# A sparse 3x3 convolution: the fifth image pair's load in two parts, later half loads moved by one or two blocks

## Chip, cores and metric

The kernel runs on one core of one Trainium2 chip. The metric is device time in microseconds (us) of the whole kernel, median over the runs.

## The reference

A 3x3 convolution with padding 1 over 16 images of 64 channels and 64 x 64 pixels, to 128 output channels. The weights are 90% zeros, but the kernel treats them as dense; what is computed is

```python
x_pad = np.pad(x, ((0, 0), (0, 0), (1, 1), (1, 1)))
for b, co, ci, kh, kw:   # x (16, 64, 64, 64) float32, weight (128, 64, 3, 3)
    output[b, co] += weight[co, ci, kh, kw] * x_pad[b, ci, kh:kh+64, kw:kw+64]
```

## The kernel before

**Pairs and blocks.** Images go in pairs: the 64 channels of two images fill 128 partitions, so there are NP = 8 pairs. A pair's 64 output rows are cut into BLOCKS = 4 blocks of ROWS = 16, which makes N = 32 blocks, counted k = 0 to 31; pair p is blocks 4p to 4p + 3. For each block three small bf16 tiles are made from the input rows: `odd` (the nine odd rows around the block, copied by ScalarE, ACT), `even` (nine even rows, by GpSimd, POOL) and `sums` (eight sums of an even and the next odd row, POOL). With weight combinations prepared at the start, TensorE makes three products of them per block: `ps[0]` from `sums` (6 matmuls), `ps[1]` from `odd` (12) and `ps[2]` or `ps[3]` from `even` (12). ACT copies `ps[0]` to `pc`; VectorE (DVE) adds `pc` to the other two and writes even and odd output rows in float32 (L288, L292).

**Loads.** Apart from the first 32 rows of pair 0, which SyncE (SP) loads in float32 at the start (L97), all input is loaded by POOL (L102), cast from float32 to bf16 on the way. `PIECES[p]` says in which row ranges a pair is loaded, each with its own semaphore `s_x[p][i]`; a fill waits for the semaphores of the rows that it reads (L118 to L153). Pair 0's rest and pairs 1 to 3 are loaded at the start. `WHEN` (L43) maps a block number k to a piece: POOL's program is one list, and behind `sums` and `even` of block k it issues that piece (L268). Pairs 3 to 7 have an input buffer of their own, so that no load waits for a buffer. From block 2 on POOL works up to two blocks ahead of TensorE: before it fills the tiles of block k it waits until TensorE is done with those of block k - 2 (L266).

**Stores.** SP stores a pair's float32 output (4 MB) when DVE is done with the pair's four blocks, pairs 6 and 7 (`HALVED`) in halves of 2 MB (L298 to L308); the very last half is issued behind the main section (L353). There are four output buffers, so DVE waits for the store of pair p - 4 before it writes pair p (L285). At the end SP waits for the semaphores of the last stores (L355).

**Order.** TensorE runs blocks in order (a loop over 16 turns of two blocks, L338 to L348); all other engines have their orders written out. A few lines carry what the change touches:

```python
    PIECES = {p: [(0, H)] for p in range(NP)}
    PIECES[0] = [(HEAD, H)]
    for p in (5, 6, 7):
        PIECES[p] = [(0, HALF * 4), (HALF * 4, H)]
    WHEN = {4: (4, 0), 7: (5, 0), 10: (5, 1), 13: (6, 0), 16: (6, 1), 20: (7, 0), 24: (7, 1)}
```

Of the kernel before, what the change touches and what calls it, by code (L numbers as in the profile page):

```python
# [16 lines left out]
HALF = 8  # L17
# [5 lines left out]
def kernel(  # L23
# [7 lines left out]
    B, C_IN, H, W = x.shape  # L31
    C_OUT, _, KH, KW = weight.shape
    assert (B, C_IN, H, W) == (16, 64, 64, 64) and (C_OUT, KH, KW) == (128, 3, 3)
    NP = B // 2
    HEAD = 32
    N = NP * BLOCKS
    HALVED = (6, 7)

    PIECES = {p: [(0, H)] for p in range(NP)}
    PIECES[0] = [(HEAD, H)]  # L40
    for p in (5, 6, 7):
        PIECES[p] = [(0, HALF * 4), (HALF * 4, H)]
    WHEN = {4: (4, 0), 7: (5, 0), 10: (5, 1), 13: (6, 0), 16: (6, 1), 20: (7, 0), 24: (7, 1)}  # L43

    def sbuf(name, shape, dtype):
        return nc.alloc_sbuf_tensor(name, shape, dtype).ap()
# [1 line left out]
    def sem(name):  # L48
        return nc.alloc_semaphore(name)
# [31 lines left out]
    s_st = [sem(f"s_st{p}") for p in range(NP)]  # L81
# [18 lines left out]
    def load(p, i=0):  # L100
        a, b = PIECES[p][i]
        nc.gpsimd.dma_start(out=xs[p][:, a:b, :], in_=pair(p)[:, a:b, :]).then_inc(s_x[p][i], 16)  # L102
# [160 lines left out]
    for k in range(1, N):  # L263
        for fill_in, product in ((fill_sums, 2), (fill_even, 6)):
            if k >= UNROLL:
                wait(g, s_pe, 6 * (k - UNROLL) + product)  # L266
            fill_in(k)
        if k in WHEN:  # L268
            load(*WHEN[k])

# [9 lines left out]
    for k in range(N):  # L280
        p, b = divmod(k, BLOCKS)
# [15 lines left out]
    s = nc.sync  # L297
# [55 lines left out]
    nc.sync.dma_start(out=into(NP - 1, H // 2, H), in_=outs[(NP - 1) % 4][:, :, H // 2 : H, :])  # L353
    with tc.tile_critical(no_gpsimd_drain=True):
        for p in range(4, NP):  # L355
            s.wait_ge(s_st[p], 16)


# [28 lines left out]
```

## Time and profile before

| | |
|---|---|
| median of 3 runs | 126.75 us (126.66 to 131.19) |
| the profiled execution | 127.12 us, of which the span from first to last instruction is 125.3 us |
| TensorE matmul busy | 110.2 us (88%), granted clock 0.962 of full speed on average |
| VectorE, POOL, ACT busy | 82.6, 63.8, 54.6 us |
| the eleven loads by POOL | 0.5 to 0.7 us of POOL each to issue; 7.8 to 19.7 us from issue to landing, the six half loads of pairs 5 to 7 12.2 us in the median |
| the stores by SP | issued at 23.1, 36.1, 49.0, 62.0, 74.9, 87.9, 94.4, 100.9, 107.4 and 114.1 us; 4 MB ones 19.2 us to landing in the median |

How to read it: busy times are those of one profiled execution, in us; the span's slices are forty equal stretches of 3.1 us, a digit is the busy share in tenths. DMA is the mean busy share of the core's 16 DMA engines, and GB/s counts the bytes that they wrote: a load that casts float32 to bf16 counts half of what it reads. "SPq" is a DMA issue in SP's queue.

### The profile page before, as it was taken

The page shows a single profiled execution, that of the slowest core. Times are in us where ns is not written, and L with a number is a line of the kernel's source. Part 1 is how long each engine was busy: PE and PEld are TensorE (multiplying, and loading weights), DVE is VectorE, ACT ScalarE, POOL GpSimd, SP SyncE. Part 2 cuts the span into 40 slices and gives each one's busy share as a digit, 9 for nine tenths or more (in the row PEclk, how much of TensorE's full clock was granted, in tenths as well). Part 3 has the DMA queues.
Part 4 walks back from the last instruction along what each step waited for, and adds up shares of the span by engine and source line. Part 5 has one row for each costly group of instructions (what it writes and reads, how often), then busy time and mean ns, then how long its engine had stood idle before and what let it go on. Part 6 is the DMA issues. An engine that isn't in the chain of part 4 may idle for free.

```text
span 125.3 us, 2489 instructions
## 1 busy us (share of the span) xinstructions
PE 110.2 (88%) x983; PEld 57.3 (46%) x983; DVE 82.6 (66%) x74; ACT 54.6 (44%) x78; POOL 63.8 (51%) x88
## 2 busy tenths in 40 slices
PE   5969999999999999999999999999999999990000
PEld 2425555555555555555555555555555555540000
DVE  0575777777777777777777777777777777773000
ACT  4525555555555555544444444444444555530000
POOL 4457557557557557556755575557555555100000
PEclk9999999999999999999999999999999999999555
DMA  3999999999999999999999999999999999999990
GB/s 110 354 221 225 215 217 212 209 165 364 379 373 362 408 331 381 392 356 364 394 371 332 430 426 345 341 436 434 362 339 413 424 408 429 429 429 421 432 408 21
DMA packets 4595, 42.79 MB, mean 342 GB/s; under 512 B 368, under 2 KB 368, under 8 KB 1392
## 3 DMA queue, kind: packets, MB, share of 16 engines
q1 hardware_dynamic: 3008, 34.90, 66.2%
q0 software_dynamic: 1584, 7.87, 31.5%
q14 instruction: 3, 0.02, 0.0%
HBM read 17.07 MB, written 33.55 MB: 404 GB/s over the span
## 4 chain that ended last, share of the span: by engine, by line
PE 82%; DVE 2%; issue 0%; DVEq 0%
PE ps L320 82%; DVE home L288 1%; DVE home L292 1%; DVEq L143 0%
## 5 line engine op out<-in xcount | busy, mean ns | idle before, releaser
L275 ACT COPY pc<-ps 128x1024 f32<-128x1024 f32 x32 | 32.4, 1012 | 51.9 <-PE ps L320 51.9
L320 PE MATMUL ps<-odd,wT 64*128 64x504 bf16 (+1 forms) x384 | 47.3, 377 | 0.0
L320 PE MATMUL ps<-even,wT 64*128 64x504 bf16 (+1 forms) x384 | 47.3, 377 | 0.0
L288 DVE TENSOR_TENSOR o<-ps,pc 128x1024 f32<-128x1024 f32 x24 | 29.4, 1225 | 19.6 <-PE ps L320 19.6
L320 PEld LDWEIGHTS ps<-even,wT 64*128 64x128 bf16 x384 | 22.0, 94 | 19.5
L320 PEld LDWEIGHTS ps<-odd,wT 64*128 64x128 bf16 x384 | 21.9, 94 | 19.5
L292 DVE TENSOR_TENSOR o<-ps,pc 128x1024 f32<-128x1024 f32 x24 | 29.4, 1224 | 0.0
L320 PE MATMUL ps<-sums,wT 64*128 64x504 bf16 (+1 forms) x192 | 26.5, 377 | 0.9 <-PEq L331 0.9
L180 POOL TENSOR_TENSOR sums<-x 128x512 bf16<-128x512 bf16 x20 | 23.1, 1157 | 0.1
L169 POOL COPY even<-x 128x576 bf16<-128x576 bf16 (+1 forms) x20 | 13.0, 649 | 19.2 <-PE ps L320 19.2
L320 PEld LDWEIGHTS ps<-sums,wT 64*128 64x128 bf16 x192 | 10.9, 94 | 11.0 <-issue 1.4
L180 POOL TENSOR_TENSOR sums<-home 128x512 bf16<-128x512 bf16 (+1 forms) x11 | 13.3, 1213 | 3.2 <-DMA home<-in_x_dram 3.1
L288 DVE TENSOR_TENSOR home<-ps,pc 128x1024 f32<-128x1024 f32 x8 | 9.8, 1225 | 6.4 <-PE ps L320 6.4
L160 ACT COPY odd<-x 128x576 bf16<-128x576 bf16 (+1 forms) x20 | 13.2, 661 | 0.0
L169 POOL COPY even<-home 128x576 bf16<-128x576 bf16 (+2 forms) x11 | 6.7, 609 | 8.2 <-PE ps L320 8.2
L292 DVE TENSOR_TENSOR home<-ps,pc 128x1024 f32<-128x1024 f32 x8 | 9.8, 1224 | 0.0
L170 POOL MEMSET even<- 128x64 bf16 x8 | 1.2, 151 | 10.8 <-PE ps L320 10.8
L236 PE MATMUL ps<-idle_rhs 128*128 128x512 bf16 x14 | 5.4, 549 | 1.4 <-DVE idle_rhs L201 1.4
L160 ACT COPY odd<-home 128x576 bf16<-128x576 bf16 (+1 forms) x10 | 6.6, 658 | 0.0
L102 POOL DMA_DIRECT2D x<-in_x_dram x8 | 4.5, 566 | 0.0
L236 PEld LDWEIGHTS ps<-idle_rhs 128*128 128x128 bf16 x14 | 1.7, 134 | 3.7 <-issue 2.1
L197 DVE CAST w_bf<-w_sb 128x192 bf16<-128x192 f32 (+1 forms) x4 | 1.1, 348 | 2.5 <-DMA w_sb<-in_weight_dram 2.5
(21 smaller groups left out, 15.2 us busy)
## 6 DMA issues: line engine op xcount, KB each, us to landing
out_dram<-o SPq DMA_DIRECT2D x5, 4096.0 KB, 19.2
out_dram<-home SPq DMA_DIRECT2D x1, 4096.0 KB, 19.3
out_dram<-o SPq DMA_DIRECT2D x2, 2048.0 KB, 14.1
out_dram<-home SPq DMA_DIRECT2D x2, 2048.0 KB, 10.9
x<-in_x_dram POOLq DMA_DIRECT2D x6, 512.0 KB, 12.2
home<-in_x_dram POOLq DMA_DIRECT2D x2, 1024.0 KB, 13.2
x<-in_x_dram POOLq DMA_DIRECT2D x2, 1024.0 KB, 16.5
home<-in_x_dram SPq DMA_DIRECT2D x1, 1024.0 KB, 6.3
```

Source lines behind the costliest of these rows:

```text
L102: nc.gpsimd.dma_start(out=xs[p][:, a:b, :], in_=pair(p)[:, a:b, :]).then_inc(s_x[p][i], 16)
L160: copy or (lambda o, i: nc.scalar.copy(out=o, in_=i)),
L169: copy or (lambda o, i: nc.gpsimd.tensor_copy(out=o, in_=i)),
L170: zero or (lambda o: nc.gpsimd.memset(o, 0.0)),
L180: engine.tensor_tensor(out=sums[k % UNROLL], in0=src[:, r0 : r0 + ROWS : 2, :], in1=src[:, r0 + 1 : r0 + ROWS : 2, :], op=ADD,).then_inc(s ...
L197: copy(out=w_bf4[:, g, a:b, :], in_=w_v[:, k : k + b - a, :]).then_inc(done, 1)
L236: t.matmul(idle_ps, idle_rhs[:, 0:128], idle_rhs, start=True, stop=True)
L275: a.copy(out=pc[k % 3], in_=ps[0]).then_inc(s_pc, 1)
L288: v.tensor_tensor(out=o[:, :, r0 : r0 + ROWS : 2, :], in0=ps[1], in1=pc[k % 3], op=ADD).then_inc(s_free, 1)
L292: v.tensor_tensor(out=o[:, :, r0 + 1 : r0 + ROWS : 2, :], in0=ps[2 + k % 2], in1=pc[k % 3], op=ADD).then_inc(s_out, 1)
L320: mm = t.matmul(into[:, n, :, c_lo:c_hi], tap(g, kw, n), src[q, i : i + HALF, c_lo + kw - 1 : c_hi + kw - 1], start=(m == 0), stop=(m == l ...
```

## The change

The load of pair 4 (the fifth) comes in two parts, rows 0 to 27 issued behind block 1 and rows 28 to 63 behind block 5 (the sixth); before, the whole was issued behind block 4. The halves of pairs 5, 6 and 7 stay halves (`H // 2` is the same 32 rows as `HALF * 4`) and are issued behind blocks 8, 11, 14, 18, 22 and 25 instead of 7, 10, 13, 16, 20 and 24. The final wait for pair 6, which is stored in two halves on one semaphore, now asks for both.

```diff
     PIECES[0] = [(HEAD, H)]
+    PIECES[4] = [(0, 28), (28, H)]
     for p in (5, 6, 7):
-        PIECES[p] = [(0, HALF * 4), (HALF * 4, H)]
-    WHEN = {4: (4, 0), 7: (5, 0), 10: (5, 1), 13: (6, 0), 16: (6, 1), 20: (7, 0), 24: (7, 1)}
+        PIECES[p] = [(0, H // 2), (H // 2, H)]
+    WHEN = {1: (4, 0), 5: (4, 1), 8: (5, 0), 11: (5, 1), 14: (6, 0), 18: (6, 1), 22: (7, 0), 25: (7, 1)}
...
         for p in range(4, NP):
-            s.wait_ge(s_st[p], 16)
+            s.wait_ge(s_st[p], 32 if p in HALVED and p < NP - 1 else 16)
```

## Prediction

> **What bounds the kernel now.** I read the page first: the slices and the queues.
>
> ```profile
> PE   5969999999999999999999999999999999990000
> DMA  3999999999999999999999999999999999999990
> q1 hardware_dynamic: 3008, 34.90, 66.2%
> q0 software_dynamic: 1584, 7.87, 31.5%
> HBM read 17.07 MB, written 33.55 MB: 404 GB/s over the span
> ```
>
> The row to see is DMA, not PE: TensorE stops at slice 36, the DMA engines run on for three more. The two queues' shares add up to 97.7% of 125.3 us, so 16 engines have some 2.9 us free in the whole span, at its two ends. q0, the loads, is counted as written, in bf16: 7.87 MB stand for twice as many bytes read. Next the chain of waits, which ends with compute:
>
> ```profile
> 8.64 102.64 PE ps L320 x948
> 111.37 1.23 DVE home L288
> 112.60 1.22 DVE home L292
> ```
>
> This is a gapless TensorE up to 111.3 us and a result at 113.8; the last store, issued at 114.12, then needs until 124.0 (9.9 us to landing) for 2.1 MB. So I asked what the DMA engines moved in chosen stretches (columns: stretch, its length, busy time of PE, its weight loads, DVE, ACT, POOL, then clock, DMA share, GB/s written):
>
> ```profile
> 9.00:24.00 15.00, 15.00 (x144) 7.91 (x139) 10.49 (x10) 8.03 (x12) 10.21 (x14) 1.00 1.02 213
> 24.00:28.00 4.00, 4.00 (x40) 2.15 (x38) 3.21 (x3) 1.65 (x3) 1.82 (x2) 1.00 1.08 178
> 28.00:30.00 2.00, 2.00 (x22) 1.03 (x18) 1.54 (x2) 1.03 (x2) 1.64 (x4) 1.00 0.93 307
> 30.00:33.00 3.00, 3.00 (x30) 1.60 (x28) 2.45 (x2) 1.34 (x2) 2.14 (x3) 1.00 1.01 429
> 35.00:39.00 4.00, 4.00 (x40) 2.17 (x38) 3.21 (x3) 1.89 (x3) 2.57 (x4) 1.00 1.00 340
> 115.00:121.00 6.00, 0.00 (x0) 0.00 (x0) 0.00 (x0) 0.00 (x0) 0.00 (x0) 0.56 1.02 430
> ```
>
> Loads alone (9 to 24) write 213, so they read 426 GB/s; stores alone go at 429 to 430. Beside a half load (35 to 39) the row says 340: the half's 1.05 MB last from 33 to about 40, 148 GB/s read and 74 written, so 266 are stores, 414 in all. The engines are thus full whatever they carry, and 50.6 MB at 0.427 take 118.6 us of the 120 between the first bytes (2.0) and the last (122.3). **The kernel is bound by DMA**; compute ends with a reserve. From 114.12 on 3.43 MB still move (0.88 us at 426, 6 at 430, then 360 and 107 GB/s for one each); 2.10 are the last store, so 1.33 MB, 3.1 us, were queued ahead of it. Two things can move the time: a stretch in which the engines have too little to do or work below their rate, or compute that comes over 3.1 us later.
>
> Single microseconds tell when a transfer's bytes appear:
>
> ```profile
> 27.00:28.00 1.00, 1.00 (x12) 0.57 (x10) 0.91 (x1) 0.31 (x1) 0.00 (x0) 1.00 0.92 205
> 28.00:29.00 1.00, 1.00 (x14) 0.51 (x10) 1.00 (x2) 0.04 (x1) 0.66 (x3) 1.00 0.86 311
> 74.00:75.00 1.00, 1.00 (x13) 0.49 (x10) 0.93 (x1) 0.65 (x1) 1.00 (x2) 1.00 0.96 410
> 75.00:76.00 1.00, 1.00 (x12) 0.55 (x10) 0.26 (x1) 0.93 (x2) 0.55 (x1) 1.00 1.02 360
> 87.00:88.00 1.00, 1.00 (x14) 0.51 (x10) 0.89 (x1) 0.69 (x1) 1.00 (x2) 1.00 1.00 426
> 88.00:89.00 1.00, 1.00 (x12) 0.52 (x10) 0.29 (x1) 0.90 (x2) 0.52 (x1) 1.00 1.02 360
> ```
>
> Loads issued at 71.09 and 84.06 pull the row down (their bytes count half) at 75 and 88: 4.0 us from issue to bytes. The first store, issued at 23.09, lifts it past 213 only in 27 to 28: some 4.2 us.
>
> **Part by part.** The POOL timeline gives the places of the issues:
>
> ```profile
> 12.14 0.66 POOL L169 COPY even<-home 128x576 bf16<-128x576 bf16 x1 [0.74 <-PE ps L320]
> 12.80 1.16 POOL L180 TENSOR_TENSOR sums<-home 128x512 bf16<-128x512 bf16 x1
> 15.38 0.15 POOL L170 MEMSET even<- 128x64 bf16 x1 [1.42 <-PE ps L320]
> 19.23 0.57 POOL L102 DMA_DIRECT2D x<-in_x_dram  x1
> ```
>
> *POOL.* One more load is issued: 0.57 us. Behind block 1 it pushes sums of block 2 from 12.80 to 13.37, done by 14.53; POOL then waits 1.42 us for TensorE anyway, and TensorE wants these sums at 8.64 + 2 x 3.24 = 15.1. Behind block 5 it starts at 22.5, again ahead of a 1.42 us wait. Nothing on the path; without that cover it would be 0.57 us of TensorE time, still inside the reserve of 3.1. The other issues trade places with an equal 0.57 elsewhere. One more semaphore and its waits for block 17 find the data long landed: nothing.
>
> *The fifth pair.* Its 2.10 MB are now queued at 12.80 (0.92 MB) and 22.5 (1.18 MB) instead of 19.23. The queue ahead is full either way: the fourth pair's load, issued at 4.11, lands at 23.8 (19.7 to landing, the longest of that line). So the early part fills no hole; it is sent at about the same moment as before. The price of smaller rows is bounded by the stretches above, 414 beside half loads against 427, 3% of 4.9 us: 0.15 us lost at most, nothing at least. I take 0.15.
>
> *First store meets the load.* From 24 to 30 the engines wrote 1.33 MB (4 x 178 + 2 x 307 KB); about 0.92 of it are the load's, so 0.41 + 1.84 = 2.25 MB really moved where 2.56 could: 0.7 us lost. The store is issued at the same 23.09 and the same load is under way, so I leave the loss as it is; its ends are all of it gone (-0.7) and as much again (+0.7).
>
> *Later halves.* Issues go from 28.98, 38.68, 48.40, 58.13, 71.09, 84.06 to behind the even fills of blocks 8, 11, 14, 18, 22, 25: 32.25, 42.0, 51.7, 64.7, 77.6, 87.4. With the median 12.2 us to landing the last three land at 76.9, 89.8, 99.6; POOL reads them at 86.70 (even, block 25), 93.84 (sums, block 28), 99.66 (even, block 29). Only the last is close, and POOL is not the limit: TensorE starts the third product of block 29 at 104.59, so with 0.66 for the copy the half may land at 103.9. Bytes are neither saved nor added, and stores take the place that a load leaves: zero, as long as a store is queued.
>
> Sum against the profiled run (127.12 us: span 125.3 and 1.8 around it): +0.15, 127.3. The median shown, 126.75, lies 0.37 below that run, so I forecast 126.9, within 0.5 either way for what two executions differ by.
>
> **Rivals.**
>
> *A, the first store's loss goes.* Row parts of 28 and 36 share the engines with the store in smaller pieces. For it: from 33 on loads in halves join a running store with no loss (340 is 414 in all). Against it: there the store was first. Minus 0.7, at most 1.1: 125.8 to 126.2.
>
> *B, the fifth pair's second part is too late.* Issued at 22.5, with 4.0 us to its bytes, it comes at 26.5. The first part starts about 23.4, takes 0.92 MB / 0.427 = 2.15 us and is through at 25.6 to 26; the store's bytes come at 27.3. Engines with nothing for 0.5 to 0.9 us: 127.4 to 127.8. Against: in 24 to 28 loads ran at 178 for 213, which stretches the first part past 26.5, and the 4.0 us were measured behind stores, not behind another load of that queue. The Trainium skill, "DMA: Bandwidth & Descriptors", section "Anatomy of one DMA", charges each such transfer some 2.0 us that do not shrink with its size; by it the split would cost 2.0 us, an estimate of 128.9, where nothing covers it. No row before shows one uncovered.
>
> *C, the stores run dry.* Place: the sixth store, issued at 87.92. Between it and the last store's issue 26.2 us pass, 11.08 MB at 0.423 (between the 414 and the 427 above), and 10.49 are supplied (4.19 and three times 2.10), so 1.33 + 11.08 - 10.49 = 1.92 MB were queued; 1.05 of them were the last half load, now issued at 87.4 with bytes at 91.4. That leaves 0.87 MB, 2.1 us. It decides at a lead of 2.1 us from a store's issue to its bytes. For it: the first store took 4.2. Against it: the weights, issued at 0.95, show bytes at 2.0, and the last store joined within its 3.1 us without a dip. At 3.1 the engines idle 1.0 us, at 4.2 until the load comes at 91.4, 1.4 us: 127.9 to 128.3. The fifth store (74.95) has 2.6 us by the same count. Idle of B and C does not add up: what is lost early lies in the queue later, and the largest counts.
>
> *D, compute stalls.* The last half lands after 103.9; each us then holds TensorE, and 3.1 are free. For 2.5 us of loss it must land at 109.5, 22 us after its issue; the longest load took 19.7, behind three others. 129.3 or more.
>
> *E, the change does nothing*: order only, the forecast's own time.
>
> **How the numbers follow.** Forecast with E 0.51, 126.9 (126.4 to 127.4); A 0.17; B 0.11; C 0.12; D 0.06; 0.03 for a gain over 2% that no row supports (all rate losses together are 1.7 us, 1.3%). From the low end of A to a little beyond C: 125.7 to 128.5. Two per cent, 2.5 us, is about what a measurement of this kernel can tell from no change. Faster by it 0.03, within 0.91, slower 0.06 (D).
>
> **What would show it.** Right: GB/s near 427 after conversion in every stretch from 30 on, TensorE without a gap from 8.6 to 111.3, the last store issued at 114.1. B: a microsecond between 25 and 28 with a low DMA share. C: a low share at 90 to 92. D: POOL's even copy of block 29 waiting for DMA. A: 24 to 30 writing over 1.4 MB. I am wrong if the DMA share drops below 0.9 for over a microsecond after 30, or if a store's lead grows with the load beside it.

## The result and the profile after

The changed kernel takes 127.05 us in the median (126.86 to 132.19, 10 runs), the kernel before 126.75; the ratio is 1.0023, 95% interval [1.0013, 1.0032]: 0.3 us slower, within 2%, against a forecast of 126.9. Runs in which the core was disturbed are left out of every ratio here; of one experiment (quarters) that leaves two runs and no interval. The profiled execution took 127.04 us with a span of 125.2.

From the page of the changed kernel, four of the rows shown before:

```profile
PE   5959999999999999999999999999999999980000
DMA  3999999999999999999999999999999999999990
q1 hardware_dynamic: 3008, 34.90, 66.4%
q0 software_dynamic: 1728, 7.87, 31.6%
```

Nothing moves in the large: the same bytes in both queues, the same full DMA row, 98.0% of the span for 97.7%. The loads have 144 packets more (128 rows and 16 completions). The chain of compute is as gapless as before:

```profile
8.34 102.64 PE ps L321 x948
111.07 1.22 DVE home L289
112.30 1.23 DVE home L293
```

It starts 0.3 us earlier and ends 0.3 us earlier (the last store is issued at 113.82 for 114.12), and the execution's own time is 127.04 for 127.12. The two profiles alone can't show a loss of 0.3 us: the profiled execution of the kernel before lies 0.37 above its median, that of the changed kernel at its median. The change also makes SP wait for both halves of pair 6; by the packet records these landed at 108.6 and 113.7 us and the last store at 123.5, so this wait does not hold the end. The stretches of the DMA engines (GB/s is the last column):

```profile
9.00:24.00 15.00, 15.00 (x142) 7.92 (x140) 10.49 (x10) 8.10 (x12) 10.48 (x15) 1.00 1.02 212
24.00:28.00 4.00, 4.00 (x40) 2.05 (x37) 3.21 (x3) 1.58 (x2) 1.82 (x2) 1.00 1.06 184
28.00:30.00 2.00, 2.00 (x22) 1.07 (x20) 1.24 (x2) 1.34 (x2) 1.82 (x3) 1.00 1.01 346
115.00:121.00 6.00, 0.00 (x0) 0.00 (x0) 0.00 (x0) 0.00 (x0) 0.00 (x0) 0.50 1.02 430
```

The place where the first store meets the load is still slow. At 90 us, where rival C looked for idle engines, there is one odd microsecond:

```profile
89.00:90.00 1.00, 1.00 (x12) 0.51 (x10) 1.00 (x2) 0.00 (x0) 0.36 (x1) 1.00 1.08 459
90.00:91.00 1.00, 1.00 (x12) 0.56 (x10) 0.83 (x1) 0.74 (x1) 1.00 (x2) 1.00 0.91 225
91.00:92.00 1.00, 1.00 (x14) 0.49 (x11) 0.38 (x1) 0.84 (x2) 0.46 (x1) 1.00 0.99 336
```

The packet records (start, size and queue of every DMA packet) split the 225 GB/s into 143 of loads and 82 of stores, where the microseconds beside it have 262 or more of stores. From 90.5 to 91.0 no packet of a store begins: the fifth store was at its end, the sixth one's bytes were not there yet, and the last half load kept the engines at 0.91.

**Two yardsticks from the packet records.** Each transfer leaves 16 packets of 4 bytes in the trace, as many as there are DMA engines. I take each for the end of one engine's part, so one can read when the middle engine and when the last engine finished the last store. And the bytes moved up to some moment, loads counted as read, can be compared between two traces; how one counts packets that are under way shifts these figures by some 0.1 us. As the reference I take the trace of late_end (below), which moves its bytes as the kernel before does and was profiled in an execution of 126.63 us.

```
                    last store done:        us of bytes behind late_end at    profiled  ratio, 95% interval
                    middle  last  apart     23     30     60     120           us
before              122.3  123.6  1.34     0.02   0.30   0.31   0.30          127.12   1
late_end            121.8  123.1  1.27     0      0      0      0             126.63   1.0004 [0.9992, 1.0016]
after (the change)  122.3  123.5  1.20     0.04   0.32   0.30   0.41          127.04   1.0023 [1.0013, 1.0032]
fifth_only          122.2  123.4  1.20    -0.10   0.24   0.32   0.34          126.93   1.0036 [1.0023, 1.0050]
fifth_split_late    122.2  123.7  1.48     0.00   0.29   0.36   0.39          127.24   1.0023 [1.0014, 1.0032]
fifth_quarters      122.3  123.5  1.24    -0.01   0.44   0.57   0.62          127.00   1.0037 [1.0020, 1.0055]
fifth_whole_early   121.8  123.1  1.31     0.12  -0.09  -0.09  -0.07          126.59   0.9999 [0.9989, 1.0008]
fourth_halves       121.9  123.4  1.52     0.07   0.07   0.06   0.07          126.93   1.0002 [0.9993, 1.0011]
later_only          121.9  123.2  1.33    -0.02  -0.08  -0.16  -0.02          126.77   1.0025 [0.9999, 1.0051]
halves_latest       121.9  123.7  1.80     0.18   0.14   0.14   0.06          127.24   1.0079 [1.0055, 1.0103]
whole               121.6  124.0  2.35     0.09   0.02  -0.13  -0.27          127.44   1.0050 [1.0034, 1.0067]
quarters            122.6  123.3  0.65     0.12  -0.02   0.13   0.62          126.62   (126.62 and 126.65)
last_quarters       122.1  122.9  0.78     0.07   0.02   0.01   0.24          126.44   0.9975 [0.9949, 1.0002]
```

In every row the profiled time is 3.4 to 3.6 us more than the moment at which the last engine is done. The end is thus the middle engine's finish plus how far the last of the 16 lags behind it. The forecast knew the first part only. Each row is one execution: the bytes and the lag say what that execution did, the ratio what many did.

### The profile page after: what moved, and what is told of

It reads as the page before. It is cut to its first block, busy times and chain, and to the rows that moved or that the text cites. A ratio compares the mean times of both kernels' runs of the same rounds, so it can differ in the third digit from the quotient of the medians.

```text
span 125.2 us, 2491 instructions
## 1 busy us (share of the span) xinstructions
PE 109.5 (88%) x983; PEld 56.5 (45%) x983; DVE 82.6 (66%) x74; ACT 54.5 (44%) x78; POOL 64.4 (51%) x89
## 4 chain that ended last, share of the span: by engine, by line
PE 82%; DVE 2%; issue 0%; DVEq 0%
PE ps L321 82%; DVE home L293 1%; DVE home L289 1%; DVEq L144 0%
## 5 line engine op out<-in xcount | busy, mean ns | idle before, releaser
L237 PE MATMUL ps<-idle_rhs 128*128 128x512 bf16 x14 | 4.8, 505 | 1.4 <-DVE idle_rhs L202 1.4
L103 POOL DMA_DIRECT2D x<-in_x_dram x9 | 5.1, 567 | 0.0
```

The costliest lines, as they stand in the source:

```text
L237: t.matmul(idle_ps, idle_rhs[:, 0:128], idle_rhs, start=True, stop=True)
```

## Experiments

**Is it bound by DMA?** The prediction rested on it, so compute was made later, and bytes were taken away.

```diff
+        if k == N - 1:
+            v.memset(scratch, 0.0)
         wait(v, s_pe, 6 * k + 6)
```

> The kernel before with a 2.1 us memset on VectorE ahead of its very last addition, so that the last store is issued at 116.2 instead of 114.1. Theory (DMA-bound): 3.1 us of stores are queued ahead of it, so no change up to a store's lead of 1.0 us, +0.1 us at a lead of 1.1 (the weights' at the start). Rival (the chain of compute ends it): +2.1 us, 1.017.

Measured: 126.87 against 126.78 us, 1.0004 [0.9992, 1.0016]. The chain of waits of that kernel shows the 2.12 us (named after the next line that DVE's queue has) right before the last addition:

```profile
7.97 102.64 PE ps L323 x948
111.95 2.12 DVEq L92
114.07 1.08 DVE home L295
```

The memset cost nothing. The last store was issued at 115.45, not at the 116.2 expected, since TensorE began 0.7 us earlier in this execution (7.97 for 8.64); the stores ahead were done on the middle engine at 116.9, with the engines at 0.98 to 1.06 all the while, so behind another store a store needs at most 1.5 us of lead.

```diff
-    nc.sync.dma_start(out=into(NP - 1, H // 2, H), in_=outs[(NP - 1) % 4][:, :, H // 2 : H, :])
+    nc.sync.dma_start(
+        out=into(NP - 1, H // 2, H - ROWS), in_=outs[(NP - 1) % 4][:, :, H // 2 : H - ROWS, :]
+    )
```

> The kernel before with the last store cut to rows 32 to 47, so that 1.05 MB of the output are left out; compute is the same. Theory (DMA-bound, the last engine sets the end): 1.05 MB at 0.427 less, -2.45 us, ratio 0.981. Rival (the chain of compute and a fixed time after it): less than 0.5 us.

Measured: 124.33 us, 0.9821 [0.9805, 0.9838]. That is -2.27 us by the ratio and -2.45 by the two medians; the forecast 0.981 lies inside. Both ways the time follows the bytes, not compute.

**Which part of the change costs?** Each part alone, and two kernels that change the number of load rows much more.

```diff
+    PIECES[4] = [(0, 28), (28, H)]
...
+    WHEN = {1: (4, 0), 5: (4, 1), 7: (5, 0), 10: (5, 1), 13: (6, 0), 16: (6, 1), 20: (7, 0), 24: (7, 1)}
```

> The kernel before with the fifth pair's load alone changed: rows 0 to 27 behind block 1, rows 28 to 63 behind block 5; the later halves stay behind blocks 7, 10, 13, 16, 20, 24. Theory (rows): the change costs time because 128 partition rows are sent as 256 shorter ones (the page counts 4739 packets for 4595: 128 and 16 completions), so this alone must give the whole loss, +0.29 us, ratio 1.002. Rival (places): the later halves cost it; then this is 1.000.

Measured: 1.0036 [1.0023, 1.0050], the whole loss.

```diff
+    WHEN = {4: (4, 0), 8: (5, 0), 11: (5, 1), 14: (6, 0), 18: (6, 1), 22: (7, 0), 25: (7, 1)}
```

> The kernel before with the halves of pairs 5 to 7 behind blocks 8, 11, 14, 18, 22, 25 and the fifth pair's load whole behind block 4. Theory (rows): no row more or less, 1.000. Rival (places): the whole loss, 1.002, and a stretch of low DMA share near 88 to 92 us.

Measured: 1.0025 [0.9999, 1.0051], too wide to tell 1.000 from the whole loss. Its trace shows no cost: no bytes behind at 120 us (-0.02), the last engine 1.33 us behind the middle one as in late_end (1.27). And the change, which has both parts, is not slower than fifth_only.

```diff
-    for p in (5, 6, 7):
-        PIECES[p] = [(0, HALF * 4), (HALF * 4, H)]
+    WHEN = {4: (4, 0), 7: (5, 0), 13: (6, 0), 20: (7, 0)}
```

> The kernel before with pairs 5, 6 and 7 loaded whole, behind blocks 7, 13 and 20: 384 rows fewer. Theory (rows): at the price that the change paid for 128 rows, 0.29 us, three times that is won: -0.87 us, ratio 0.993; half of it if the price was for the place beside the first store. Rival (places): no change, 1.000, as these loads ran beside stores before too.

```diff
-        PIECES[p] = [(0, HALF * 4), (HALF * 4, H)]
+        PIECES[p] = [(r, r + H // 4) for r in range(0, H, H // 4)]
...
-            load(*WHEN[k])
+            p, i = WHEN[k]
+            if p == 4:
+                load(p)
+            else:
+                load(p, 2 * i)
+                load(p, 2 * i + 1)
```

> The kernel before with pairs 5 to 7 loaded in quarters of 16 rows, two issued back to back where a half was: 768 rows more, POOL issues six loads more. Theory (rows): six times 0.29 us, +1.7 us, ratio 1.014. Rival (places): 1.000, since the bytes come at the same times.

Both went against the theory of rows. With 384 rows fewer, whole is slower: 127.43 us, 1.0050 [1.0034, 1.0067]. With 768 rows more, quarters has only the two runs 126.62 and 126.65, no slower than the 126.74 before. The table says why. In bytes moved the rows do count: -0.27 us at 120 for whole, +0.62 for quarters, some 0.1 us for 128 rows. But the last engine goes the other way: 2.35 us behind the middle one in whole, 0.65 in quarters. This is what the end of whole looks like:

```profile
121.00:122.00 1.00, 0.00 (x0) 0.00 (x0) 0.00 (x0) 0.00 (x0) 0.00 (x0) 0.50 0.45 188
122.00:123.00 1.00, 0.00 (x0) 0.00 (x0) 0.00 (x0) 0.00 (x0) 0.00 (x0) 0.50 0.06 25
123.00:124.00 1.00, 0.00 (x0) 0.00 (x0) 0.00 (x0) 0.00 (x0) 0.00 (x0) 0.50 0.06 25
```

A DMA share of 0.06 and 25 GB/s are one engine of 16 (427 / 16 = 26.7), alone at work for two microseconds. In quarters the engines finish nearly together:

```profile
121.00:122.00 1.00, 0.00 (x0) 0.00 (x0) 0.00 (x0) 0.00 (x0) 0.00 (x0) 0.50 1.04 442
122.00:123.00 1.00, 0.00 (x0) 0.00 (x0) 0.00 (x0) 0.00 (x0) 0.00 (x0) 0.50 0.47 197
123.00:124.00 1.00, 0.00 (x0) 0.00 (x0) 0.00 (x0) 0.00 (x0) 0.00 (x0) 0.50 0.00 0
```

**Place or split, in the fifth pair?** The lag of the last engine does not explain the change itself (1.20 us, a little less than before). What fifth_only and the change share in the table is a step between 23 and 30 us: 0.3 us of bytes lost there and not regained. The trace of the kernel before has this step too (0.02 to 0.30), in an execution 0.37 us above its median, so the traces of before and after don't tell the two kernels apart here. Two kernels separate the place from the split.

```diff
-    WHEN = {4: (4, 0), 7: (5, 0), ...
+    WHEN = {1: (4, 0), 7: (5, 0), ...
```

> The kernel before with the fifth pair's load whole, but behind block 1: the place without the shorter rows. If the price of fifth_only (ratio 1.0036) is the place: 1.0036 here too. If it is the shorter rows: 1.000. A price set by which of the 16 engines is left behind would not follow either: between 0.998 and 1.004.

```diff
+    PIECES[4] = [(0, 28), (28, H)]
...
+    WHEN = {4: [(4, 0), (4, 1)], 7: [(5, 0)], 10: [(5, 1)], 13: [(6, 0)], 16: [(6, 1)], 20: [(7, 0)], 24: [(7, 1)]}
...
-            load(*WHEN[k])
+            for piece in WHEN[k]:
+                load(*piece)
```

> The kernel before with the fifth pair's load in 28 and 36 rows, both parts issued behind block 4 where the whole was: shorter rows, old place. Theory (short rows where the first store arrives): the loads of 23 to 27 us fall from the 180 to 201 GB/s of whole loads to about 160, and the price of fifth_only returns: 1.0025 to 1.0045. Rival (two issues apart in time, or the lead of the second one): 1.000, as nothing is issued apart here.

Measured: whole and early 0.9999 [0.9989, 1.0008], split at the old place 1.0023 [1.0014, 1.0032]. The place is free, the split costs all of it. The stretch from 23 to 27 us in two kernels with the fifth pair's load whole, fifth_whole_early and whole, then in two with it split, fifth_split_late and the change:

```profile
23.00:27.00 4.00, 4.00 (x40) 2.14 (x38) 2.93 (x3) 2.08 (x3) 1.94 (x3) 1.00 1.05 201
```

```profile
23.00:27.00 4.00, 4.00 (x40) 2.17 (x38) 2.69 (x3) 2.32 (x4) 2.17 (x3) 1.00 1.02 178
```

```profile
23.00:27.00 4.00, 4.00 (x42) 2.06 (x38) 2.60 (x3) 2.34 (x4) 2.26 (x3) 1.00 1.06 160
```

```profile
23.00:27.00 4.00, 4.00 (x40) 2.12 (x38) 2.66 (x3) 2.34 (x4) 2.75 (x3) 1.00 1.08 161
```

The four figures can't be compared as they stand, because GB/s counts stores in full and loads by half. By the packet records 33 of the 201 are stores and 4 of the 178; the two split kernels have loads alone there. The first store's moment shifts with TensorE's start (8.07, 8.31, 8.40 and 8.34 us): it was issued at 22.52, 22.75, 22.84 and 22.79, and its first bytes come at 26.6, 26.7, 27.3 and 27.2. So loads did not fall from 201 to 160. With loads counted as read, the four rows stand for 369, 352, 320 and 322 GB/s. All kernels with the fifth pair whole lie at 340 to 369 there, the kernel before at 344; fifth_only has 307. Over the four microseconds the engines are busy in all of them (1.02 to 1.08): with the split they move fewer bytes in as much busy time.

From 23 to 30 us the table says the same: the four kernels with the fifth pair split fall back by 0.28 to 0.45 us, those with it whole by none (-0.21 to 0.00), apart from the trace before with its 0.28. In that trace the first store came latest of all (issued at 23.09, bytes at 27.3); a late store alone does not make the step, for whole, with 22.75, has none, and fifth_only, with 22.29, has it. That the split costs is shown by the ratios of many runs; the step is where the traces put it, and a kernel without the split can have it too.

**Only there, and by how much?**

```diff
+    PIECES[4] = [(r, r + H // 4) for r in range(0, H, H // 4)]
...
+    WHEN = {1: [(4, 0), (4, 1)], 3: [(4, 2), (4, 3)], 7: [(5, 0)], ...
```

> The kernel before with the fifth pair's load in quarters of 16 rows, two behind block 1 and two behind block 3: three times the added rows of the change, all queued early. Theory (short rows where the first store arrives): more loss than the split in two, at three times its 0.35 us about +1.0 us, 1.008. Rival (a fixed price for splitting, or for the second part's issue behind block 5): 1.0036 or 1.000.

```diff
+    PIECES[3] = [(0, 28), (28, H)]
...
     for p in (1, 2, 3):
         load(p)
+    load(3, 1)
```

> The kernel before with the fourth pair's load, which moves at 18 to 23 us and meets no store, in 28 and 36 rows; the fifth stays whole. Theory (the price is paid only where the first store arrives): 128 rows at the 0.10 us that whole and quarters show in the bytes moved, 1.001 at most. Rival (every added 128 rows cost the same): 1.0036.

Measured: the fourth pair split the same way costs nothing, 1.0002 [0.9993, 1.0011]. The fifth in quarters costs 1.0037 [1.0020, 1.0055], not the 1.008 expected, and just the 1.0036 that the rival of a fixed price for splitting named. Its trace has 144 GB/s from 23 to 27, all loads, and 0.44 us of bytes behind at 30. So the price is tied to the fifth pair, and it does not grow in proportion to the rows. Of the 0.62 us at 120, a third comes after 30 us. Whether the shorter rows or the additional transfers cost is not separated, as every split here has both. That it is the arrival of the first store which makes the fifth pair dear fits the time of the step, but no run moved that store: it is not shown, and why the work is slower just there stays open.

**Stores that run dry.** Rival C, with more halves held back than in the change:

```diff
-    ... 13: (6, 0), 16: (6, 1), 20: (7, 0), 24: (7, 1)}
+    ... 13: (6, 0), 20: (6, 1), 24: (7, 0), 26: (7, 1)}
```

> The kernel before with the last three halves behind blocks 20, 24 and 26 (16, 20, 24 before): the queue of stores is 2.45 us shorter at the sixth store's issue (87.9 us) than with the change, which had 2.1 us left, so the engines must run dry there, some 0.4 us until the half issued at 84.1 sends bytes. Theory (stores run dry): +0.4 us or more, 1.003 or more, with a DMA share under 0.9 in 86 to 88 or 90 to 92. Rival (order of bytes is free): 1.000 and a full DMA row.

Measured: 127.54 us, 1.0079 [1.0055, 1.0103]: 1.0 us by the ratio, 0.8 by the medians.

```profile
74.00:75.00 1.00, 1.00 (x12) 0.56 (x10) 0.41 (x1) 1.00 (x2) 1.00 (x1) 1.00 1.04 410
75.00:76.00 1.00, 1.00 (x14) 0.49 (x11) 0.78 (x1) 0.41 (x1) 0.03 (x1) 1.00 0.95 258
76.00:77.00 1.00, 1.00 (x12) 0.54 (x10) 1.00 (x2) 0.00 (x0) 0.55 (x1) 1.00 1.06 221
...
87.00:88.00 1.00, 1.00 (x12) 0.56 (x10) 0.37 (x1) 1.00 (x2) 1.00 (x1) 1.00 0.86 238
88.00:89.00 1.00, 1.00 (x14) 0.51 (x10) 0.81 (x1) 0.38 (x1) 0.00 (x0) 1.00 1.03 217
```

The stores run out twice, at 75 and at 87 (221 and 217 GB/s are loads but for 16), but the engines hardly stop: 0.86 in the worst microsecond. In all, no bytes are behind at 120 us (0.06). The loss of this execution is in the lag: the last engine ends 1.80 us after the middle one, 0.53 more than in late_end, which covers the 0.6 us between their times (127.24 and 126.63). The profiled execution is the quickest of its six runs; what the others lost beyond it no trace shows.

**A version that beats both?** The table suggested finer rows only at the end, where they might level the engines.

```diff
+    PIECES[7] = [(r, r + H // 4) for r in range(0, H, H // 4)]
+    WHEN = {4: [(4, 0)], 7: [(5, 0)], ... 20: [(7, 0), (7, 1)], 24: [(7, 2), (7, 3)]}
```

> The kernel before with the last pair alone in quarters, two issued where a half was: 256 rows more. Theory (bytes and the last engine): +0.2 us of bytes moved, and the last of the 16 engines less far behind the middle one than the 1.2 to 1.35 us of half loads (0.65 in quarters): between 0.996 and 1.000. Rival (rows alone): 1.0015 to 1.003.

Measured: 126.44 us in the median against 126.74, 0.9975 [0.9949, 1.0002]. 0.24 us of bytes behind, the last engine only 0.78 behind the middle one. It is the quickest kernel of the study by its median, and faster than the changed one, but its interval just takes in 1: a gain over the kernel before isn't shown. (Ten of the eleven runs in the ratio lie at 126.36 to 126.61, one at 127.41.)

## Why the prediction was right, and where it was not

The forecast was 0.15 us up, to 126.9, and the kernel came out 0.3 us up, at 127.05, inside the range of rival E. The kind of bound and the sign were reasoned; that the number is so near is partly luck. E means that only the order changes, which is not what happened, and of the two terms that failed, below, one was too small and the other put at zero, in a margin of 0.5 us that had room for both.

*DMA sets the end: right.* 2.1 us of added compute cost nothing, 1.05 MB less gave 2.27 us. What it left out is that the slowest of 16 engines, not their sum, is the end. This made no difference for the change (1.20 us of lag for 1.27 to 1.34) but it turns the sign for whole, and in quarters it cancels the 0.62 us of bytes.

*POOL, one more issue: free, but misread.* I took the even fill at 12.14 for block 1; it is that of block 2. The issue stands three microseconds earlier, as the timeline after shows:

```profile
9.75 0.23 POOL L170 COPY even<-home 128x64 bf16<-128x64 bf16 x1
9.93 0.57 POOL L103 DMA_DIRECT2D x<-in_x_dram  x1
10.52 1.17 POOL L181 TENSOR_TENSOR sums<-home 128x512 bf16<-128x512 bf16 x1
11.84 0.66 POOL L170 COPY even<-home 128x576 bf16<-128x576 bf16 x1
```

It uses up most of a wait for TensorE of 0.74 us there and harms nothing, and fifth_whole_early shows that a load issued at this place is free.

*The fifth pair: the term that was mis-sized.* +0.15 us at most, from 3% of 4.9 us for shorter rows beside stores. Measured, fifth_only costs 1.0036 and fifth_split_late 1.0023: 0.45 and 0.3 us. The rate by which I priced it was taken at 35 to 39 us, where a store runs already; there, by whole and quarters, 128 rows cost only 0.1 us. The price was in the stretch from 23 to 30 us, which I chose to leave as it is.

*The first store meets the load: the failed choice.* I held its 0.7 us loss unchanged, with ends of -0.7 and +0.7. Against late_end it got worse by some 0.3 us (0.24 to 0.32 of bytes behind at 30 in the three kernels with the fifth pair in 28 and 36 rows), inside these ends. The size was misread as well: the packet records give the loads 0.77 MB from 24 to 30, not the 0.92 that I took, so 2.10 MB moved and 1.1 us was lost. And the trace I read it from was itself behind there, by 0.30 us, while its median execution is 0.37 us quicker; that is why the two profiled executions look alike in this stretch. Rival A had the mechanism with the sign reversed: smaller pieces made that stretch slower, not faster. Its sign was badly chosen too: from 24 to 30 the changed kernel wrote 4 x 184 + 2 x 346 = 1.43 MB, over the 1.4 that I named for A, but late_end, with whole rows, wrote 1.47. GB/s counts stores in full, so this sum follows the moment at which the first store's bytes come.

*Later halves: zero, as far as shown.* later_only leaves 1.000 and 1.005 open; its trace has no bytes behind and the usual lag.

*B* is out: the second part followed the first without a hole (no microsecond from 24 to 28 has a DMA share under 0.94), and fifth_split_late, where both were queued together, costs the same as the change. What the Trainium skill charges for a transfer ("DMA: Bandwidth & Descriptors", section "Anatomy of one DMA", about 2.0 us whatever its size) was fully covered in fourth_halves, at 1.0002. *C* came close: no store packet began for half a microsecond at 90, and the DMA share stayed at 0.91. In halves_latest, one step further, the stores ran out for longer and the kernel is 1.0 us slower, but not by idle engines, as I had worked it out. *D* did not occur: POOL's even copy of block 29 starts at 99.36 after 1.42 us of waiting for TensorE, not for DMA.

## What to carry to other kernels

When the DMA row is full from end to end, count bytes first, and then ask which engine finishes last: an average rate can't see one straggler of sixteen. A whole load issued nine microseconds earlier into a full queue cost nothing here (0.9999), and a split load cost nothing in one place (1.0002) and 0.3 us in another, where the first store's bytes arrive. So price a moved or split transfer with the rows of its own moment and not of the steady state, and read these with loads and stores apart when GB/s counts them differently. And when a median differs by 0.3%, first see where each profiled execution lies among its own runs: here the trace before was the slower one.

## What was not expected of the hardware

In all thirteen traces of the table the last DMA engine ended 0.65 to 2.35 us after the middle one. In nine of them it is alone, over 0.7 us behind the next; in fifth_quarters two are late, by 1.13 and 1.24 us. The Trainium skill, "DMA: Bandwidth & Descriptors", section "Latency and other measured facts", says that two of the engines are usually slower in traces and offers as its best guess the descriptor rings of loads issued by GpSimd. That single engines are slower agrees with the traces, whose packet records do not say which they are. The guess finds no support here: the kernel with the most load packets, quarters (2448), had the smallest lag and whole (1152) the largest, in one trace each. What makes the lag is open.
